# A decoder layer with routed experts on one core: rows of the modulation split between two engines, attention cut into pieces, half of one row moved into the routing, two output tiles lent to the weight stream

## The chip, the cores and the metric

The kernel runs on one core of a Trainium2 chip. The metric is the device time of one execution in microseconds (us); three runs gave 1640.99, 1641.44 and 1648.26 us, median 1641.44. What a run takes is decided by five engines with a queue each (TensorE, called PE in the profile; VectorE, DVE; ScalarE, ACT; GpSimd, POOL; SyncE, SP, which here only issues transfers) and by the 16 DMA engines that bring weights from memory.

## The reference, cut to what matters

One layer over 256 tokens of width 2048, all in float32:

```python
mod = (silu(c) @ ada_w + ada_b)                 # 6 rows of 2048
sh1, sc1, g1, sh2, sc2, g2 = split(mod, 6)
h = rmsnorm(x, norm1_g) * (1 + sc1) + sh1
x = x + g1 * hybrid_mixer(h)                    # h @ w_in -> heads -> @ w_out
h = rmsnorm(x, norm2_g) * (1 + sc2) + sh2
x = x + g2 * hierarchical_moe(h)                # 32 experts, 2 for each token
return rmsnorm(x, final_norm_g)
```

`hybrid_mixer` projects h to 5392 columns and feeds three groups of heads: a dilated-window attention (columns aq, ak, av), a gated delta rule with a short convolution (bq, bk, bv, a gate bz, and 16 gate columns bb, ba), and a grouped-query window attention (cq, ck, cv). Their outputs, side by side, go through `w_out`. Each expert is a gated MLP with two 2048x512 matrices in and one 512x2048 out, 12 MB of weights; all 32 experts are computed.

## The kernel before, in words

**Weights as a stream.** All big weights pass as tiles of 128 x 2048 float32 (1 MB) through rings of buffers. `Stream` (L114) keeps a queue of loads and a set of free slots: a load is issued on SP's queue when a slot is free (`pump`), the next tile is taken with `get`, and `done` frees its slot. `grow` adds slots, `retire` takes them out. There are two streams: `st` for nearly everything, and `st2`, with two slots, for the rows of the modulation that are needed later. The order of loads within a stream is the order of `add` (L472 to L484): the rest of the projection, the 16 tiles of `w_out`, then the 384 tiles of the experts. Each engine's instructions are put in order when the program is built, by a planner that follows the written order where nothing forces another; on the chip each queue runs strictly in order.

**First part.** The rows sh1 and sc1 and the columns bq, bk, bv are computed in six slices of the 2048 inputs (`SLICES`, L38): `ada_items` and `win_items` are merged, `win_tile` (L357) splits each float32 weight tile into a rounded half and a rest (`split`, L281: the rounding on ACT, the subtraction on DVE or POOL), multiplies in three products (`mm3`) and adds each slice's result to the sum in SBUF (`evac`, L267, on DVE). The 16 gate columns are multiplied there too (`gate_columns`, L370), tokens on the rows and 16 columns to stream.

**Second part.** All other columns, in pairs of 256 (`win_pair`, L391), use the finished h. In the written order come: `delta()` (L676), the long chain of the delta rule (conv, gates, a block inverse in six levels L812 to L842, states, outputs `ob`); then `use(merge(a_cols, rows_q[0:24]))`, `attention(0)`, the columns of c with 12 rows' tiles, `attention(1)`, and the columns bz with 20 (L937 to L941). `rows_q` are the 64 tiles of the rows g1, sh2, sc2 and g2, 16 each, multiplied on PE by `row_tile` (L425) in four groups of 32 output rows. Then `delta_out` (L885) and `wout_part` (L913), in two rounds of four.

**Routing and experts.** After `w_out`, x is normalised again, group and expert are chosen (L998 to L1055), and the chosen tokens are gathered by matrix products (`Slots`, L1083). The experts go in pairs: `hidden` (16 tiles a pair), `second` (8 tiles a pair), and `scatter` back into x. Slots of `st` in this stage: three of `ring1`, its two side slots (L951), four of `ring2` (L954), three of `ring3` (L1013) and the two buffers of `xa`, `h2` (L1061). `new_y` (L1211) takes four tiles of 128 x 1024 for the outputs of a pair.

What sets the room around the change:

```python
st.retire(*spare)            # L575
for s in side:
    st.retire(s, to=st2)
st.grow((wk, "rx"))          # one more slot until L947
...
st.grow(*slots(ring3, "rd", R4))                     # L1013
...
st.grow(*((cst, f"h2{b}") for b in range(NB)))       # L1061
```

Of the kernel before, what the change touches and what calls it, by code (L numbers as in the profile page):

```python
# [8 lines left out]
F32 = mybir.dt.float32  # L9
F32R = mybir.dt.float32r  # L10
# [6 lines left out]
P = 128  # L17
# [21 lines left out]

PAIRS = [c for a, e in ((O_AQ, O_BQ), (O_CQ, N_IN), (O_BZ, O_BB)) for c in range(a, e, 256)]  # L40

EARLY = ([("ada", s, k0, nk, q) for k0, nk in SLICES for s in range(2) for q in range(nk)]
         + [("b", k0, nk, c) for k0, nk in SLICES for c in range(O_BQ, O_BZ, 2048 // nk)]
         + [("pair", c, h) for c in PAIRS for h in range(2)]
# [4 lines left out]
def hybrid_moe(ctx: ExitStack, tc: tile.TileContext, x, c, norm1_g, norm2_g, early, ada_w, ada_b, w_bb,  # L49
# [154 lines left out]
    def win_items(j):  # L204
        k0, nk = SLICES[j]
        return [(early_load("b", k0, nk, c), lambda t, a=(k0, nk, c): win_tile(*a)(t)) for c in range(O_BQ, O_BZ, 2048 // nk)]

# [18 lines left out]
    for nk, r in ((4, 4), (2, 8)):  # L226
# [6 lines left out]
        for k0, n in SLICES:  # L233
            if n == nk:
# [10 lines left out]
    CH = [("aq0", 0, 2), ("aq1", 2, 2), ("ak0", 4, 2), ("ak1", 6, 2), ("bq", 8, 4), ("bk", 12, 4),  # L245
          ("bv0", 16, 4), ("bv1", 20, 4), ("cq0", 24, 2), ("cq1", 26, 2), ("ck", 28, 1)]
# [110 lines left out]
    def win_tile(k0, nk, c0):  # L357

        def chans(w, cc, m):

            h = hs[k0]
            p = bank("w")
            for u in range(2):
                for kt in range(nk):
                    mm3(p[:, 256 * u:256 * u + 256], [x[:, kt, cc + P * u:cc + P * (u + 1)] for x in w],
                        [x[:, kt] for x in h], kt == 0, kt == nk - 1)
            t, i = chan[m]
            evac(t[:, i:i + 2].rearrange("p m b t -> p (m b t)"), p, k0)

        def gate_columns():  # L370
            h = hs[k0]
            for b in range(NB):
                p = bank("w")
                for kt in range(nk):
                    mm3(p[:, 0:16], [x[:, kt, P * b:P * (b + 1)] for x in h], [x[:, k0 // P + kt] for x in wbb],
                        kt == 0, kt == nk - 1)
                evac(tok[:, b, K_BB:K_BB + 16], p[:, 0:16], k0)

        def f(t):
            t = t.rearrange("p (k n) -> p k n", k=nk)  # L380
            n = 1024 // nk
            for a in range(0, 2048 // nk, n):
                w = split(t[:, :, a:a + n], nk, 0)
                for z in range(0, n, 256):
                    chans(w, z, 8 + (c0 - O_BQ + a + z) // P)
            if c0 == O_BQ:
                gate_columns()
        return f
# [33 lines left out]

    rowp = {}

    def row_tile(i, kt):  # L425
        def f(t):
            if kt == 0:
                rowp[i] = bank("r", name="prow2")
            for g in range(4):
                mm(rowp[i][32 * g:32 * g + 32, :], csil[:, kt, 3 - i:35 - i], t[:, 512 * g:512 * (g + 1)],  # L430
                   start=(kt == 0), stop=(kt == 15))
# [18 lines left out]

    rows_q = [(ada_rows(i, kt), row_tile(i, kt)) for i in range(4) for kt in range(KT)]

# [16 lines left out]
    a_cols, c_cols, z_cols = ([x for c0 in range(a, e, 256) for x in on(st, win_pair(c0))]  # L469
                              for a, e in ((O_AQ, O_BQ), (O_CQ, N_IN), (O_BZ, O_BB)))  # L470
# [105 lines left out]
    for s in side:  # L576
        st.retire(s, to=st2)
    st.grow((wk, "rx"))
    use(first[-8:])
# [82 lines left out]
    def attention(grp):  # L662
        if grp:
            swap_keys()
            clo = ep_tile("av", 4, F32R)
        for j in range(2):
            ms = (2 * j, 2 * j + 1)
            sd = [attn_scores(grp, m) for m in ms]
            pair = (ep_tile(f"cq{j}", 2, F32R), clo[:, 2 * j:2 * j + 2]) if grp else \
                (ep_tile(f"aq{j}", 2, F32R), ep_tile(f"ak{j}", 2, F32R))  # L670
            for i, m in enumerate(ms):
                mix[m if grp == 0 else 12 + m] = tuple(t[:, i] for t in pair)
                attn_values(grp, m, *sd[i])


    def delta():  # L676
# [269 lines left out]
    g1hl = halves(scratch(dt=F32R), scratch(dt=F32R), mrow)  # L946
    st.retire((wk, "rx"))  # L947
# [341 lines left out]
    with tc.For_i(0, nov, 1):  # L1289
# [113 lines left out]
```

## Time and profile before

| | |
|---|---|
| median of three runs | 1641.44 us |
| profiled execution, whole | 1645.27 us |
| its span, first to last instruction | 1643.4 us |
| PE busy | 1545.9 us (94%) |
| DVE busy | 672.1 us (41%) |
| ACT busy | 398.6 us (24%) |
| POOL busy | 182.8 us (11%) |
| bytes moved | 573.76 MB, mean 349 GB/s |

An engine's busy time is the union of its instructions' times. A float32 product appears as two instructions, and products overlap in the array, so the mean duration of one is longer than the time between two: what a group costs is its busy time over its count. The line of a matrix product is always that of the helper `mm` (L65); what it belongs to is told by its output and input tiles.

### The profile page before, as it was taken

How to read it: one execution, taken by the hardware profiler on the slowest of the kernel's cores; microseconds unless marked ns; L12 is line 12 of the kernel's file. 1: busy time of each engine (PE TensorE's matmuls, PEld its weight loads, DVE VectorE, ACT ScalarE, POOL GpSimd, SP SyncE). 2: the span in 40 equal slices, each digit the busy share in tenths (PEclk: the TensorE clock that was granted, in tenths of full speed). 3: DMA queues.
4: the chain of work that ended last, by engine and by line, in shares of the span. 5: the costliest groups of instructions: out<-in, count | busy, mean ns of one | idle time of the engine just before them, and what ended most of it. 6: DMA issues, size and time to landing. Idle time of an engine off the chain costs nothing. (4 is left out here: it accounts for less than half of the span.)

```text
span 1643.4 us, 23829 instructions
## 1 busy us (share of the span) xinstructions
PE 1545.9 (94%) x10064; PEld 945.0 (58%) x10064; DVE 672.1 (41%) x1138; ACT 398.6 (24%) x683; POOL 182.8 (11%) x104
## 2 busy tenths in 40 slices
PE   5899899999999999799999999999999999999895
PEld 3678767898877667544544545445445445445433
DVE  3534854334433544423432533344244234235324
ACT  3323563344345334210110110111011101101102
POOL 1111222352222432000000000000000000000000
PEclk8999999999999999799999999999999999999998
DMA  9986457634589894699999999999999999999995
GB/s 392 408 329 237 162 206 293 246 155 161 225 309 315 308 369 178 232 397 421 420 419 421 421 420 421 421 420 420 421 420 421 420 421 421 421 421 421 420 420 218
DMA packets 82437, 573.76 MB, mean 349 GB/s; under 512 B 9740, under 2 KB 10100, under 8 KB 13336
## 3 DMA queue, kind: packets, MB, share of 16 engines
q1 hardware_dynamic: 82080, 572.02, 86.6%
q8 instruction: 81, 1.33, 0.3%
q10 hardware_dynamic: 248, 0.19, 0.0%
q14 instruction: 28, 0.23, 0.0%
HBM read 570.07 MB, written 2.10 MB: 348 GB/s over the span
## 5 line engine op out<-in xcount | busy, mean ns | idle before, releaser
L65 PE MATMUL u<-ring,xg 128*64 128x512 f32 x2048 | 485.9, 604 | 7.8 <-DMA ring<-in_expert_gu_dram 7.8
L65 PEld LDWEIGHTS u<-ring,xg 128*64 128x64 f32 x2048 | 134.3, 137 | 236.1 <-issue 190.5
L65 PE MATMUL d<-ring,hidT 128*64 128x256 f32 x2048 | 238.1, 382 | 10.5 <-DMA ring<-in_expert_dn_dram 8.9
L65 PE MATMUL w<-hx,stg 128*128 128x256 f32 x1392 | 197.1, 293 | 9.8 <-ACT stg L289 3.1
L65 PEld LDWEIGHTS w<-hx,stg 128*128 128x128 f32 x1392 | 176.6, 194 | 41.8 <-issue 24.3
L65 PEld LDWEIGHTS d<-ring,hidT 128*64 128x64 f32 x2048 | 144.0, 137 | 90.9 <-issue 10.3
L290 POOL TENSOR_TENSOR stg<-ring,stg 128x1024 fp32r<-128x1024 f32 x53 | 128.3, 2421 | 410.5 <-ACT stg L289 367.3
L289 ACT CAST stg<-ring 128x1024 fp32r<-128x1024 f32 x116 | 121.2, 1047 | 187.7 <-PE w L65 152.4
L1190 DVE TENSOR_TENSOR xt<-xt,s 128x512 f32<-128x512 f32 x120 | 82.6, 688 | 165.2 <-PE s L65 164.4
L290 DVE TENSOR_TENSOR stg<-ring,stg 128x1024 fp32r<-128x1024 f32 x63 | 82.2, 1306 | 104.5 <-ACT stg L289 103.7
L1174 DVE SCALAR_TENSOR_TENSOR z<-d,gs,g2b 64x512 f32<-64x512 f32 x120 | 90.0, 750 | 76.1 <-PE d L65 74.2
L65 PE MATMUL prow<-ring,csil 128*32 128x512 f32 (+1 forms) x896 | 113.3, 566 | 0.3 <-DVE csil L180 0.3
L1272 POOL TENSOR_TENSOR xf<-xt,fgb 128x1024 f32<-128x1024 f32 x1 | 2.4, 2377 | 954.9 <-SPq L1289 954.9
L1107 DVE TENSOR_TENSOR xg<-g,sh2c 128x512 f32<-128x512 f32 x64 | 43.6, 691 | 136.8 <-PE u L65 75.7
L65 PEld LDWEIGHTS w<-stg,hx 128*128 128x128 f32 x672 | 83.6, 189 | 22.3 <-issue 18.0
L65 PE MATMUL w<-stg,hx 128*128 128x256 f32 (+1 forms) x672 | 96.1, 288 | 0.0
L1146 ACT ACTIVATE hid<-u 64x512 f32<-64x512 f32 x32 | 18.9, 590 | 286.7 <-PE u L65 276.5
L65 PEld LDWEIGHTS s<-yah,wt 128*128 128x128 f32 x120 | 22.6, 188 | 97.6 <-issue 58.8
L1177 ACT CAST yah<-z 64x512 fp32r<-64x512 f32 x60 | 37.0, 617 | 166.8 <-DVE z L1174 166.8
L1147 DVE TENSOR_TENSOR hid<-hid,u 64x512 f32<-64x512 f32 x32 | 22.1, 690 | 134.0 <-ACT hid L1146 133.8
L65 PE MATMUL g<-oh,h2hi 128*128 128x256 f32 x256 | 70.2, 307 | 5.5 <-DVE xg L1107 4.8
L1121 ACT CAST wt<-t 128x512 fp32r<-128x512 f32 x16 | 9.4, 587 | 233.7 <-PE s L65 222.6
(387 smaller groups left out, 1704.6 us busy)
## 6 DMA issues: line engine op xcount, KB each, us to landing
ring<-in_expert_gu_dram SPq DMA_DIRECT2D x256, 1024.0 KB, 19.8
ring<-in_expert_dn_dram SPq DMA_DIRECT2D x128, 1024.0 KB, 19.8
ring<-in_early_dram SPq DMA_DIRECT2D x90, 1024.0 KB, 8.2
ring<-in_ada_w_dram SPq DMA_DIRECT2D x64, 1024.0 KB, 5.7
xt<-in_x_dram SPq DMA_DIRECT2D x8, 512.0 KB, 6.3
out_dram<-xt SPq DMA_DIRECT2D x8, 256.0 KB, 4.4
fgb<-in_final_norm_g_dram SPq DMA_DIRECT2D x1, 1024.0 KB, 19.8
rw<-in_router_w_dram SPq DMA_DIRECT2D x1, 320.0 KB, 5.2
```

Source lines behind the costliest of these rows:

```text
L65: return T.matmul(o, lhsT, rhs, start=start, stop=stop, skip_group_check=True)
L289: S.copy(hi, src)
L290: (G if nsplit[0] % GS[part] == GS[part] - 1 else V).tensor_tensor(lo, src, hi, op=ALU.subtract)
L1107: V.tensor_tensor(self.xg[:, 2 * q:2 * q + 2, 0:w], p[:, 0:2 * w].rearrange("p (k s) -> p k s", k=2), sh2c.rearrange("p n k -> p (n k)")[: ...
L1121: S.copy(self.wt.rearrange("p h b t -> p (h b t)"), p)
L1146: S.activation(hid[64:128], p[0:64], AF.Silu)
L1147: V.tensor_tensor(hid[0:64], hid[64:128], p[64:128], op=ALU.mult)
L1174: V.scalar_tensor_tensor(o.rearrange("p (n j) -> p n j", n=m), pd[q, 0:256 * m].rearrange("p (n j) -> p n j", n=m), gs[q, h, u:u + 1], g2h ...
L1177: S.copy(ys[h][q, c], o)
L1190: V.tensor_tensor(x1[n][:, b], x1[n][:, b], p, op=ALU.add)
L1272: G.tensor_tensor(xf, x1[0], fgb[:, None, 0:512].to_broadcast([P, NB, 512]), op=ALU.mult)
```

## The change

Four things.

1. The columns aq and ak join bq, bk and bv in the six slices; of `win_pair`'s columns av, cq, ck, cv and bz stay. The gate columns are multiplied the other way round (16 output rows, 256 tokens to stream) and turned back at the start of `delta`; cv is computed like ck and turned in `swap_keys`.
2. The rows g1 and sc2 (i = 0 and 2) are accumulated on DVE, tile by tile, into a buffer `racc`, and summed over the 128 rows by one set of four products at the end. The rows sh2 and g2 stay on PE. They alternate in the queue, and are spread evenly over the steps of the second part, among which `attention` now yields piece by piece. `racc` takes the room of the slot `rx`.
3. Of g2's 16 tiles the last 8 leave `st2`, and stand in `st` between `w_out` and the experts. They are multiplied after the routing is written, and g2 is spread over the tokens' rows behind the first expert's products instead of in `w_out`'s second round.
4. The expert outputs become two tiles of 8 KB a row in a pool of their own. Each serves `st` as a slot once, before it holds outputs.

```diff
-PAIRS = [c for a, e in ((O_AQ, O_BQ), (O_CQ, N_IN), (O_BZ, O_BB)) for c in range(a, e, 256)]
+PAIRS = [c for a, e in ((O_AV, O_BQ), (O_CQ, N_IN), (O_BZ, O_BB)) for c in range(a, e, 256)]
+SLICED = [(O_BQ, O_BZ), (O_AQ, O_AV)]
...
         def gate_columns():
             h = hs[k0]
-            for b in range(NB):
-                p = bank("w")
-                for kt in range(nk):
-                    mm3(p[:, 0:16], [x[:, kt, P * b:P * (b + 1)] for x in h], [x[:, k0 // P + kt] for x in wbb],
-                        kt == 0, kt == nk - 1)
-                evac(tok[:, b, K_BB:K_BB + 16], p[:, 0:16], k0)
+            p = bank("w")
+            for kt in range(nk):
+                mm3(p[0:16, 0:256], [x[:, k0 // P + kt] for x in wbb], [x[:, kt] for x in h], kt == 0, kt == nk - 1)
+            evac(bbT, p[0:16, 0:256], k0)
...
-    KINDS = [(O_AQ, O_AV, "chan", 0), (O_AV, O_BQ, "av", 0), (O_BQ, O_BZ, "chan", 8), (O_BZ, O_BB, "tok", K_BZ),
-             (O_CQ, O_CV, "chan", 24), (O_CV, N_IN, "tok", K_CV)]
+    KINDS = [(O_AV, O_BQ, "av", 0), (O_BZ, O_BB, "tok", K_BZ), (O_CQ, N_IN, "chan", 24)]
...
+        def on_dve(t):
+            if kt == 0:
+                rowp[i] = wk.tile([P, D], F32, name="racc", tag="racc")
+            acc = rowp[i]
+            for h in range(2):
+                c = slice(1024 * h, 1024 * (h + 1))
+                if kt == 0:
+                    V.tensor_scalar(acc[:, c], t[:, c], csil[:, kt, 3:4], None, op0=ALU.mult)
+                else:
+                    V.scalar_tensor_tensor(acc[:, c], t[:, c], csil[:, kt, 3:4], acc[:, c], op0=ALU.mult, op1=ALU.add)
             if kt == 15:
+                rowp[i] = bank("d", name="prow2")
+                for g in range(4):
+                    mm(rowp[i][32 * g:32 * g + 32, :], onec[:, 3 - i:35 - i], acc[:, 512 * g:512 * (g + 1)])
+        def f(t):
+            (on_pe if i % 2 else on_dve)(t)
+            if kt == (7 if i == 3 else 15):
                 V.tensor_tensor(mrow, mrow, rowp.pop(i), op=ALU.add)
...
-    rows_q = [(ada_rows(i, kt), row_tile(i, kt)) for i in range(4) for kt in range(KT)]
+    rows_q = [(ada_rows(i, kt), row_tile(i, kt)) for i0 in (0, 2) for kt in range(KT) for i in (i0, i0 + 1)
+              if i < 3 or kt < 8]
...
+    for kt in range(8, KT):
+        st.add(ada_rows(3, kt))
     for e in range(0, NE, 2):
...
-    st.grow((wk, "rx"))
     use(first[-8:])
...
-    use(merge(a_cols, rows_q[0:24]))
-    attention(0)
-    use(merge(c_cols, rows_q[24:36]))
-    attention(1)
-    use(merge(z_cols, rows_q[36:56]))
+    parts = [attention(grp) for grp in range(2)]
+    steps = a_cols + merge(c_cols, parts[:1] * 8) + merge(z_cols, parts[1:] * 8)
+    for step in merge(steps, rows_q[0:48]):
+        if isinstance(step, tuple):
+            use([step])
+        else:
+            next(step)
...
-        use(rows_q[56 + 2 * n:56 + 2 * n + 2])
+        use(rows_q[48 + 2 * n:48 + 2 * n + 2])
...
-        pg = bank("w")
-        spread2(pg, g1hl, 3, n)
-        S.copy(g2b[:, ns], pg)
...
+    for t in ("yh", "yl"):
+        st.grow((yp, t))
+        st.retire((yp, t))
...
+    p = bank("s", 1)
+    for kt in range(8):
+        t = st.get()
+        for g in range(4):
+            mm(p[32 * g:32 * g + 32, :], csil2[:, kt, 0:32], t[:, 512 * g:512 * (g + 1)], start=(kt == 0), stop=(kt == 7))
+        st.done()
+    g2r = mp.tile([P, 512], F32, name="g2r", tag="hid", bufs=1)
+    V.tensor_tensor(g2r, mrow, p, op=ALU.add)
+    g2hl = halves(*(mp.tile([P, 512], F32R, name="g2hl", tag="z") for _ in range(2)), g2r)
+
+    def spread_g2(n):
+        p = bank("s", 1)
+        spread2(p, g2hl, 3, n)
+        S.copy(g2b[:, 512 * n:512 * (n + 1)], p)
...
-    behind = []
+    behind = [lambda n=n: spread_g2(n) for n in range(4)]
...
-        yh, yl = new_y(F32R, "h"), new_y(F32R, "l")
+        yh, yl = new_y(F32R, "yh"), new_y(F32R, "yl")
```

## Rows read from the trace of the kernel before

**Rows 1.** The page: the span in 40 equal slices of 41 us; TensorE's granted clock and the share of the DMA engines in tenths, then GB/s.

```profile
PE   5899899999999999799999999999999999999895
PEclk8999999999999999799999999999999999999998
DMA  9986457634589894699999999999999999999995
GB/s 392 408 329 237 162 206 293 246 155 161 225 309 315 308 369 178 232 397 421 420 419 421 421 420 421 421 420 420 421 420 421 420 421 421 421 421 421 420 420 218
```

**Rows 2.** Busy time of each engine by stage (slices, second part, `w_out`, routing and first products, experts, end): length, busy us and instruction count of each engine, granted clock, DMA share, GB/s.

```profile
0.00:190.00 190.00, 163.05 (x1337) 130.66 (x1338) 88.06 (x168) 63.32 (x99) 29.43 (x25) 0.93 0.81 319
190.00:535.00 345.00, 339.31 (x2643) 272.87 (x2643) 149.16 (x273) 162.38 (x312) 107.83 (x60) 0.99 0.64 234
535.00:662.00 127.00, 125.81 (x614) 86.23 (x612) 58.16 (x70) 48.59 (x65) 42.88 (x18) 1.00 0.73 276
662.00:706.00 44.00, 34.44 (x166) 20.92 (x168) 18.10 (x51) 9.01 (x16) 0.24 (x1) 0.81 0.70 261
706.00:1618.00 912.00, 873.60 (x5246) 428.17 (x5242) 346.80 (x558) 108.90 (x178) 0.00 (x0) 0.99 1.01 420
1618.00:1644.00 26.00, 9.70 (x66) 6.14 (x64) 11.79 (x23) 6.43 (x14) 2.38 (x1) 0.77 0.36 113
```

**Rows 3.** TensorE's groups in the first 700 us, shapes kept apart: operation, out<-in, contraction rows * output rows, in partitions x elements, count, busy us, mean ns of one, idle before.

```profile
L65 PE MATMUL w<-hx,stg 128*128 128x256 f32 x1392 | 197.1, 293 | 9.8 <-ACT stg L289 3.1 <-DVE hx L352 2.8 <-DVE stg L290 1.5
L65 PE MATMUL prow<-ring,csil 128*32 128x512 f32 x640 | 90.8, 605 | 0.0
L65 PE MATMUL w<-wbb,hx 128*128 128x16 f32 x96 | 12.9, 259 | 0.0
L65 PE MATMUL w<-stg,hx 128*128 128x128 f32 x96 | 12.3, 276 | 0.0
L65 PE MATMUL w<-g1hl,identr 32*128 32x512 f32 x16 | 5.8, 441 | 0.0
```

**Rows 4.** DVE's and POOL's lines: durations of one in ns (least, median, most), first and last start, shape.

```profile
L1060 DVE SCALAR_TENSOR_TENSOR h2lo<-xa,r,h2hi x8: 735/748/752, 666.1 to 671.8; 128x512 fp32r<-128x512 f32 x8
L290 DVE TENSOR_TENSOR stg<-ring,stg x63: 1209/1225/3124, 26.7 to 652.7; 128x1024 fp32r<-128x1024 f32 x63
L931 DVE TENSOR_TENSOR xt<-xt,w 128x512 f32<-128x512 f32 x16 | 10.4, 679 | 0.0
L271 DVE TENSOR_TENSOR bq<-bq,w x10: 680/688/689, 56.8 to 182.2; 128x512 f32<-128x512 f32 x10
```

**Rows 5.** The chain of the delta rule and what ends beside it: lines with their durations, first and last start.

```profile
L691 ACT ACTIVATE ct<-bq,cw x4: 493/496/504, 183.0 to 184.2; 128x256 f32<-128x256 f32 x4
L803 DVE SCALAR_TENSOR_TENSOR R<-d,beta,qk x16: 336/341/351, 263.5 to 290.4; 128x128 f32<-128x128 f32 x16
L834 DVE TENSOR_TENSOR Tm<-Tm,d x20: 391/422/424, 305.6 to 379.2; 128x256 f32<-128x256 f32 x20
L880 DVE TENSOR_TENSOR ob<-ob,d x2: 671/680/689, 431.2 to 444.0; 128x512 f32<-128x512 f32 x2
L417 ACT COPY tok<-w x10: 257/367/378, 451.3 to 533.9; 128x256 f32<-128x256 f32 x8, 128x128 f32<-128x128 f32 x2
```

**Rows 6.** Busy time of three stretches, columns as in rows 2.

```profile
175.00:225.00 50.00, 44.19 (x321) 36.69 (x321) 39.62 (x73) 34.22 (x51) 12.12 (x7) 0.93 0.54 183
225.00:662.00 437.00, 433.61 (x3028) 332.77 (x3026) 180.18 (x290) 183.60 (x336) 141.73 (x73) 1.00 0.68 252
...
670.00:675.00 5.00, 0.00 (x0) 0.00 (x0) 4.73 (x23) 0.83 (x2) 0.00 (x0) 0.50 0.45 152
```

**Rows 7.** DVE operations of the chain and of the attention with two inputs in SBUF: durations as in rows 4.

```profile
L696 DVE SCALAR_TENSOR_TENSOR ct<-bv,cw,ct x24: 470/475/2597, 212.6 to 233.0; 128x255 f32<-128x255 f32 x8, 128x254 f32<-128x254 f32 x8, 128x253 f32<-128x253 f32 x8
L635 DVE SCALAR_TENSOR_TENSOR sc<-sc,cntA x16: 276/415/2274, 286.5 to 409.1; 128x128 f32<-128x128 f32 x8, 128x256 f32<-128x256 f32 x8
```

**Rows 8.** SP's queue: issues of expert loads around the routing (start, length of the merged piece, count).

```profile
600.25 0.43 SPq L191 DMA_DIRECT2D ring<-in_expert_gu_dram  x1
601.28 84.39 SPq L191 DMA_DIRECT2D ring<-in_expert_gu_dram  x14
653.99 0.33 SPq L191 DMA_DIRECT2D ring<-in_expert_gu_dram  x1
661.39 0.81 SPq L191 DMA_DIRECT2D ring<-in_expert_gu_dram  x2
671.91 0.99 SPq L191 DMA_DIRECT2D ring<-in_expert_gu_dram  x2
685.34 0.33 SPq L191 DMA_DIRECT2D ring<-in_expert_gu_dram  x1
```

**Rows 9.** The instructions in order of time in the routing: start, length, engine, line, out<-in, count, idle time before and what ended it.

```profile
666.58 1.93 PE L65 MATMUL d<-rw,xT 128*128 128x40 f32 x8 [0.75 <-ACT xT L993]
675.06 1.06 PE L65 MATMUL t<-Ae,before 128*128 128x32 f32 x4 [6.55 <-DVE Ae L1049]
677.33 0.58 PE L65 MATMUL g<-oh,h2hi 128*128 128x256 f32 x1 [0.78 <-DVE oh L1093]
683.37 3.65 PE L65 MATMUL u<-ring,xg 128*64 128x512 f32 x16
```

**Rows 10.** The tiles of the rows: TensorE's products on them between 450 and 535 us, and what SP's queue waited for before it could load them (us in total, times, longest).

```profile
L65 PE MATMUL prow<-ring,csil 128*32 128x512 f32 x136 | 18.1, 605 | 0.0
SPq L188 <- PE prow L65: 235.9, 56, 17.2
```

More of the change, by code (lines that the diff above doesn't have):

```diff
@@ L38 @@
 SLICES = [(0, 2), (256, 2), (512, 4), (1024, 4), (1536, 2), (1792, 2)]
-PAIRS = [c for a, e in ((O_AQ, O_BQ), (O_CQ, N_IN), (O_BZ, O_BB)) for c in range(a, e, 256)]
+PAIRS = [c for a, e in ((O_AV, O_BQ), (O_CQ, N_IN), (O_BZ, O_BB)) for c in range(a, e, 256)]
+SLICED = [(O_BQ, O_BZ), (O_AQ, O_AV)]
 EARLY = ([("ada", s, k0, nk, q) for k0, nk in SLICES for s in range(2) for q in range(nk)]
-         + [("b", k0, nk, c) for k0, nk in SLICES for c in range(O_BQ, O_BZ, 2048 // nk)]
+         + [("b", k0, nk, c) for k0, nk in SLICES for a, e in SLICED for c in range(a, e, 2048 // nk)]
          + [("pair", c, h) for c in PAIRS for h in range(2)]
@@ L180, in hybrid_moe @@
     V.tensor_copy(csil[:, :, 3], pt[:, 0:KT])
+    csil2 = cst.tile([P, 8, 36], F32, name="csil2")
+    V.tensor_copy(csil2, csil[:, 8:16])
     def early_load(*key):
@@ L205, in win_items @@
         k0, nk = SLICES[j]
-        return [(early_load("b", k0, nk, c), lambda t, a=(k0, nk, c): win_tile(*a)(t)) for c in range(O_BQ, O_BZ, 2048 // nk)]
+        return [(early_load("b", k0, nk, c), lambda t, a=(k0, nk, c): win_tile(*a)(t)) for s, e in SLICED for c in range(s, e, 2048 // nk)]
     def on(s, items):
@@ L245, in hybrid_moe @@
     CH = [("aq0", 0, 2), ("aq1", 2, 2), ("ak0", 4, 2), ("ak1", 6, 2), ("bq", 8, 4), ("bk", 12, 4),
-          ("bv0", 16, 4), ("bv1", 20, 4), ("cq0", 24, 2), ("cq1", 26, 2), ("ck", 28, 1)]
+          ("bv0", 16, 4), ("bv1", 20, 4), ("cq0", 24, 2), ("cq1", 26, 2), ("ck", 28, 1), ("cv", 29, 1)]
     chan = {}
     K_BZ, K_BB, K_CV = 0, 1024, 1040
-    KINDS = [(O_AQ, O_AV, "chan", 0), (O_AV, O_BQ, "av", 0), (O_BQ, O_BZ, "chan", 8), (O_BZ, O_BB, "tok", K_BZ),
-             (O_CQ, O_CV, "chan", 24), (O_CV, N_IN, "tok", K_CV)]
+    KINDS = [(O_AV, O_BQ, "av", 0), (O_BZ, O_BB, "tok", K_BZ), (O_CQ, N_IN, "chan", 24)]
     def ep_tile(tag, n, dt=F32):
@@ L259, in hybrid_moe @@
             chan[m0 + i] = (t, i)
+    bbT = ep.tile([P, 256], F32, name="bbT")[0:16]
     av = ep.tile([P, NB, 512], F32, name="av", tag="av")
@@ L384, in f @@
                 for z in range(0, n, 256):
-                    chans(w, z, 8 + (c0 - O_BQ + a + z) // P)
+                    chans(w, z, (c0 + a + z) // P - (O_BQ // P - 8 if c0 >= O_BQ else 0))
             if c0 == O_BQ:
@@ L423, in hybrid_moe, with on_pe @@
     rowp = {}
+    onec = ep.tile([P, 36], F32, name="onec")
+    V.memset(onec, 0.0)
+    V.memset(onec[:, 3:4], 1.0)
     def row_tile(i, kt):
-        def f(t):
+        def on_pe(t):
             if kt == 0:
@@ L430, in f @@
                 mm(rowp[i][32 * g:32 * g + 32, :], csil[:, kt, 3 - i:35 - i], t[:, 512 * g:512 * (g + 1)],
-                   start=(kt == 0), stop=(kt == 15))
-            if kt == 15:
+                   start=(kt == 0), stop=(kt == (7 if i == 3 else 15)))
+        def on_dve(t):
[8 more added lines that the diff above has]
+                    V.scalar_tensor_tensor(acc[:, c], t[:, c], csil[:, kt, 3:4], acc[:, c], op0=ALU.mult, op1=ALU.add)
+            if kt == 15:
+                rowp[i] = bank("d", name="prow2")
[4 more added lines that the diff above has]
+            if kt == (7 if i == 3 else 15):
                 V.tensor_tensor(mrow, mrow, rowp.pop(i), op=ALU.add)
@@ L469, in hybrid_moe @@
     a_cols, c_cols, z_cols = ([x for c0 in range(a, e, 256) for x in on(st, win_pair(c0))]
-                              for a, e in ((O_AQ, O_BQ), (O_CQ, N_IN), (O_BZ, O_BB)))
+                              for a, e in ((O_AV, O_BQ), (O_CQ, N_IN), (O_BZ, O_BB)))
     w_items = [(early_load("out", n, q), None) for qs in ((0, 3), (1, 2)) for n in range(4) for q in qs]
@@ L593, in swap_keys @@
     def swap_keys():
+        p = bank("a")
+        for b in range(NB):
+            T.transpose(p[:, P * b:P * (b + 1)], head(29)[:, b], ident)
+        S.copy(tok[:, :, K_CV:K_CV + 128], p[:, 0:256].rearrange("p (b n) -> p b n", b=NB))
         kd = wk.tile([P, NB, P], F32, name="kswap")
@@ L667, in attention @@
             ms = (2 * j, 2 * j + 1)
-            sd = [attn_scores(grp, m) for m in ms]
+            sd = []
+            for m in ms:
+                sd.append(attn_scores(grp, m))
+                yield
             pair = (ep_tile(f"cq{j}", 2, F32R), clo[:, 2 * j:2 * j + 2]) if grp else \
@@ L673, in attention @@
                 attn_values(grp, m, *sd[i])
+                yield
     def delta():
@@ L701, in delta @@
         conv(1)
+        pt = bank("d")
+        for b in range(NB):
+            T.transpose(pt[:, 16 * b:16 * (b + 1)], bbT[:, P * b:P * (b + 1)], ident[0:16, 0:16])
+        V.tensor_copy(tok[:, :, K_BB:K_BB + 16], pt[:, 0:32].rearrange("p (b n) -> p b n", b=NB))
         bb = tok[:, :, K_BB:K_BB + 8]
@@ L946, in hybrid_moe @@
     g1hl = halves(scratch(dt=F32R), scratch(dt=F32R), mrow)
-    st.retire((wk, "rx"))
     for n in range(4):
         wout_part(n, (0, 3), g1hl, tmp.tile([P, 2, 384], F32, name="g1s", tag="pT").rearrange("p u s -> p (u s)")[:, 0:512])
-        use(rows_q[56 + 2 * n:56 + 2 * n + 2])
+        use(rows_q[48 + 2 * n:48 + 2 * n + 2])
     st.grow(*side)
@@ L1014, in hybrid_moe @@
     mp = ctx.enter_context(tc.tile_pool(name="moe", bufs=2, side="right", reuse_waits="tile"))
+    yp = ctx.enter_context(tc.tile_pool(name="yp", bufs=1, side="right", reuse_waits="tile"))
+    for t in ("yh", "yl"):
+        st.grow((yp, t))
+        st.retire((yp, t))
     psum = ctx.enter_context(tc.tile_pool(name="mps", bufs=1, space=bass.MemoryType.PSUM, reuse_waits="tile"))
@@ L1204, in squares @@
             if n == 3 and b:
-                y = mp.tile([P, 1024], F32, name="sqv", tag="yal", bufs=1)[:, 0:512]
+                y = new_y(F32, "yl")[0][:, 0:512]
                 V.scalar_tensor_tensor(y, x1[n][:, b], 0.0, x1[n][:, b], op0=ALU.add, op1=ALU.mult, accum_out=ss3[:, b, n:n + 1])
@@ L1211, in new_y @@
     def new_y(dt, s):
-        return tuple(mp.tile([P, 1024], dt, name=f"y{h}{s}", tag=f"y{h}{s}", bufs=1) for h in "ab")
+        t = yp.tile([P, 2, 1024], dt, name=s, tag=s)
+        return t[:, 0], t[:, 1]
     ovn, ovs, ove = small("ovn", [P, NE]), small("ovs", [P, NE]), small("ove", [P, NE])
@@ L1272, in scaled @@
         G.tensor_tensor(xf, x1[0], fgb[:, None, 0:512].to_broadcast([P, NB, 512]), op=ALU.mult)
-    ys = new_y(F32, "h")
+    ys = new_y(F32, "yh")
     for n in range(4):
@@ L1314, in hybrid_moe @@
         sl.back(0)
-        ys = new_y(F32, "h")
+        ys = new_y(F32, "yh")
         G.memset(ys[0][64:128], 0.0)
```

## Prediction

> **What bounds the kernel now.** I read the page's 40 slices first, then the busy time by stage, then TensorE's groups, and last SP's issues around the routing. The reader is to see two kernels in one. From about 706 us to 1618 us the DMA engines run at 420 GB/s without a gap [rows 1, 2]: a tile of 1.049 MB every 2.495 us, and no engine's work there can move the end unless it stops the stream. Before 662 us it is TensorE: from 190 to 662 us it is busy 465.1 of 472 us while DMA has a share of 0.64 and 0.73 [rows 2]. Between the two, from 662 to 706 us, neither is full: DMA has 0.70 [rows 2], because 14 slots are filled by 672.9 us and the next load is issued only at 685.34 us, when the first expert tile has been used [rows 8]. So the end is the moment at which `w_out` is done (R, 662 us), plus the loads still to come, plus the gaps in them. The change works on all three.
>
> **The sum, on TensorE before R.** Costs per instruction are busy time over count [rows 3].
>
> Rows g1 and sc2 leave TensorE: 32 tiles of 8 instructions at 90.8/640 = 0.142 us, 36.3 us. The two final sums bring back 2 x 8 x 0.142 = 2.3 us. Net -34.0.
>
> Half of g2's row leaves: 8 tiles of 8 instructions, -9.1.
>
> The gate columns: 96 products of 16 columns cost 12.9 us, 48 of 256 columns take their place. No row shows 16 output rows; the nearest, 128 output rows and 256 columns, is 197.1/1392 = 0.142 us, so 6.8 us. With 0.3 us of transposes, -5.8. Bounds: the 96 old ones halved (6.5) and twice the price (13.6), -6 to +1.
>
> cv: 96 products of 128 columns, 12.3 us, become 48 of 256, 6.8 us, and 0.3 us of transposes, -5.2.
>
> g2's spread: half of a group of 16, 5.8/2, -2.9; it goes behind the first expert's products, in the DMA-bound stage.
>
> The columns aq and ak move and don't shrink: 4 pairs x 96 products x 0.142 = 54.4 us go from the second part into the slices. There 8 more tiles are loaded, 20 us of DMA in a stage of 190 us with a share of 0.81 [rows 2], and DVE adds 20 sums of 0.69 us [rows 4], 14 us where it is busy 88 of 190. I cost both at nothing; without that cover they would be 20 us.
>
> Sum: -34.0 - 9.1 - 5.8 - 5.2 - 2.9 = -57.0 us.
>
> **What it costs on DVE.** 64 operations over 1024 columns with two inputs in SBUF. No row shows this one. The subtraction of the same shape takes 1.225 us, and an operation with a column of factors 0.748 against 0.679 us at 512 columns [rows 4], so 1.225 + 0.07 = 1.29 us, 83 us in all. DVE's load between the slices and R was 207 us of 472 [rows 2]; it becomes about 280 of 366. That alone still fits. What counts is who stands behind them in DVE's queue. The chain of the delta rule begins with the first convolution at 183.0 and ends with the last `ob` at 444.7, 261.7 us, while the gate's last columns came at 533.9 [rows 5]: 89 us of cover. Afterwards the chain starts at 183.0 + 54.4 - 5.8 = 231.6 and would end at 493; the columns end at 533.9 - 5.8 - 5.2 - 36.3 + 1.1 (32 of 56 rows' tiles fewer on TensorE in this stretch, one final sum) = 488. The cover is gone, and what lengthens the chain is late in `delta_out` and after it. By the code 118 of its steps are DVE's (48 convolution taps, 28 where the blocks are set up, 24 in the levels, 4 of scaling, 14 in the last loop). 48 of the 64 row operations are spread over this stretch, 48 x 1.29 / 257 = 24% of the time; a step finds one in its way that often and waits half of it, 0.155 us, 118 times: 18 us. Bounds: nothing, or a gain of a few us, if the chain is shorter with less other work on TensorE, which was 100% busy beside it; and 12% of 366 us, 43 us, from the stretch in which DVE was busy 39.6 of 50 us and TensorE lost 5.8 [rows 6]. I take 18, near the middle: in the rest of the stage, with DVE at 41%, TensorE lost only 3.4 of 437 us [rows 6].
>
> In this case's rows an operation of DVE with two SBUF inputs, 0.475 or 0.415 us as a rule, took up to 2.597 and 2.274 us [rows 7], which is about a POOL subtraction longer. The Trainium skill (SBUF — State Buffer, Who interferes with whom) says that such an operation and a GpSimd one that reads SBUF exclude each other, and the second blocks fully. The trace agrees for single ones. All 64 row operations have two SBUF inputs but the first of each row, and POOL is busy 151 of 472 us [rows 2], so by the rule a third of them would wait some 1.2 us, 25 us more on DVE, and the 18 us would be 24; but the subtraction on DVE, with the same two inputs, shows a median of 1.225 us against a least of 1.209 [rows 4], so I leave the sum at 18.
>
> **What the loads cost.** Before, nine expert tiles were issued by 654 us, three at 661 to 662, two at 672 [rows 8]. Now eight of the first nine slots hold g2's tiles: 8 more expert tiles are to come after R, +19.9 us. Against it the gap closes: at R there are five slots (three of `ring3`, two of the outputs), at R + 10 two more, and the eight of g2 as TensorE takes them in its idle 6.55 us before the ranks and 0.78 us before the gather [rows 9]. Five and two tiles keep DMA busy for 17.5 us, the eight for 20 more. So the 44 us at 0.70 become full: -44 x (1 - 0.70/1.01) = -13.5 us. The two lent slots are what bridges R + 12.5 to R + 17.5; their worth, 5 us, is inside this. Net +6.4. Bounds: +19.9 if the gap stays, -13.5 if g2's tiles are used before R and their slots are free for experts. g2's products need 9.1 us in 7.3 us of idle time, twice that at the granted clock of 0.50 (1.2 GHz) that the idle TensorE has at 670 us [rows 6]; the first expert would start 2 to 11 us later after R, behind which the loads wait for nothing, since 16 slots are there. I cost that at nothing.
>
> Total: -57.0 + 18 + 6.4 = -32.6 us. The profiled execution took 1645.3 us, of which 1643.4 are span, and would take 1612.7; the median is 3.8 us lower, so 1609 us.
>
> **Rivals.** (a) DVE's queue costs nothing: -57.0 + 6.4, 1591 us. For it speaks that DVE has 86 us to spare and TensorE's other work can fill the waits; against it the lost cover. (b) The two slots of `st2` pace the rows. Before, 136 products are 17 tiles in 85 us, 5.0 us each, and SP waited 4.2 us for the slot, 56 times [rows 10]; 48 tiles at 5.0 us are 240 us in a stretch of 257, but a tile that DVE uses is held 2.6 us and not 1.1, and if it waits behind other work, 6 us each make 288 us: 31 over, and SP's queue holds the other loads behind. With TensorE's own small loss, -57 + 6.4 + 34, 1625 us; with the 18 as well, 1640. (c) The end on the other side: DVE's strict order makes the chain the bound. If the row operations stand ahead of every DVE step, half a one each time, 118 x 0.645 = 76 us: -57 + 6.4 + 76, 1667 us. It decides from 0.43 us a step, 51 us in all; for it speaks that a row operation takes three times a level's step of 0.42 us [rows 5], against it that they cover a quarter of the stretch. (d) Part three doesn't do what it says: g2's tiles are used late, their slots come late and the gap stays at 13.5 us: 1622 us; that lies within the forecast's own range.
>
> **How the numbers follow.** The forecast with (d) gets 0.57 (1594 to 1624), (a) 0.20, (b) 0.13, (c) 0.10. About 0.5% is what a measurement of this kernel can tell from no change, so faster is below 1633.2 and slower above 1649.6. Faster: 0.57 + 0.20 + half of (b), 0.83. Within: the other half of (b) and the low end of (c), 0.08. Slower: 0.09. The range reaches from 1582, a little below (a) where the chain shortens, to 1637, which leaves out the upper end of (b) and (c).
>
> **What would show it.** Right: the first convolution near 232 us, `ob` complete near 511, `w_out` done near 624, and from there DMA at 1.0 without the gap at the first expert; no products of `prow` for g1 and sc2. The DVE part is wrong if TensorE's idle time in the second part is under 5 us (then (a)) or the chain takes over 300 us (then (c)); SP waiting over 6 us for each row's tile would show (b). The load part is wrong if DMA still falls under 0.9 between R and the first expert. The prediction fails as a whole if TensorE's busy time before R is not some 57 us shorter, or if the expert stage no longer runs at 420 GB/s.

## The result, and the profile after

The changed kernel took 1657.7 us (median of five, 1655.96 to 1659.2) against 1641.44 us: the ratio is 1.0086, with a 95% interval of 1.0062 to 1.0110. The prediction was 1609 us, faster, with a range of 1582 to 1637. It was wrong in sign.

The page of the changed kernel, the same lines as [rows 1], with DVE's; a slice is 41.4 us:

```profile
PE   5999989999993599999999999999999999999995
...
DVE  3455689853255654423532443344244234235324
...
PEclk8999999999995699999999999999999999999998
DMA  9997686762147884999999999999999999999995
GB/s 394 374 356 257 238 304 242 294 223 104 61 151 281 291 319 151 376 420 420 420 420 421 420 420 420 420 420 420 420 420 420 420 420 420 420 420 420 421 420 213
```

The reader is to see a hole that the kernel before did not have: TensorE at 3 and 5 tenths in the 13th and 14th slice, and, ahead of it, DMA at 2, 1 and 4 tenths in the 10th to 12th slice. The stages, columns as in [rows 2] (slices; the delta rule; from its end to the first use of g1; `w_out`; routing and first products):

```profile
0.00:211.00 211.00, 189.10 (x1578) 152.33 (x1582) 108.10 (x186) 76.33 (x110) 39.72 (x29) 0.97 0.83 323
211.00:495.00 284.00, 273.80 (x2082) 235.19 (x2080) 179.54 (x297) 153.38 (x300) 103.64 (x56) 0.98 0.54 196
495.00:554.00 59.00, 19.32 (x80) 4.74 (x80) 29.90 (x36) 2.76 (x6) 1.04 (x1) 0.53 0.77 278
554.00:669.00 115.00, 106.66 (x450) 77.67 (x450) 67.99 (x78) 39.40 (x52) 34.74 (x14) 0.95 0.68 250
669.00:706.00 37.00, 33.98 (x198) 17.97 (x200) 18.83 (x52) 10.01 (x19) 0.24 (x1) 0.91 1.00 401
```

In the 59 us from 495 to 554 us TensorE is busy 19 us, at a granted clock of 0.53, near the lower of its two levels (0.50, 1.2 GHz); DVE is busy 30 us and no other engine more than 3. The last row is the routing, and there DMA has 1.00, against 0.70 before [rows 2]: that part came as forecast. The instructions in order of time around the hole say what happens:

```profile
342.33 1.27 DVE L447 SCALAR_TENSOR_TENSOR racc<-ring,csil,racc 128x1024 f32<-128x1024 f32 x1
...
492.43 1.05 PE L67 MATMUL d<-t,qk 128*128 128x128 f32 x8
493.41 1.06 PE L67 MATMUL prow<-racc,onec 128*32 128x512 f32 x8
496.22 0.67 DVE L456 TENSOR_TENSOR mrow<-mrow,prow 128x512 f32<-128x512 f32 x1
496.82 1.40 DVE L445 TENSOR_SCALAR racc<-ring,csil 128x1024 f32<-128x1024 f32 x2
499.54 1.94 PE L67 MATMUL prow<-ring,csil 128*32 128x512 f32 x8 [5.06 <-DVE mrow L456]
...
553.84 0.69 DVE L456 TENSOR_TENSOR mrow<-mrow,prow 128x512 f32<-128x512 f32 x1 [2.93 <-PE prow L67]
554.62 0.62 ACT L463 CAST t<-mrow 128x512 fp32r<-128x512 f32 x1 [43.65 <-DVE mrow L456]
```

DVE has finished row 0 in `racc` at 343.6 us. Its sum over the 128 rows (`prow<-racc,onec`) comes 150 us later, at 493.41, right behind the last product of the delta rule (`d<-t,qk`). Until then `racc` is taken, so row 2 can't begin, and row 1's bank `r` is taken as well, since row 1 is added to `mrow` after row 0 (498.8 us); so row 3 can't begin either. The first tiles of rows 2 and 3 are used at 496.82 and 499.54 us. By then all other work of the second part is done, and `w_out`'s first round needs g1 out of `mrow`, which is read only after row 3's sum: ACT waits 43.65 us for it.

### The profile page after: what moved, and what is told of

It is laid out like the page before. It is cut to its first block, busy times and chain, and to the rows that moved or that the text cites. A ratio compares the mean times of both kernels' runs of the same rounds, so it can differ in the third digit from the quotient of the medians.

```text
span 1654.1 us, 23250 instructions
## 1 busy us (share of the span) xinstructions
PE 1511.8 (91%) x9732; PEld 922.3 (56%) x9732; DVE 763.3 (46%) x1226; ACT 397.7 (24%) x679; POOL 181.8 (11%) x101
## 5 line engine op out<-in xcount | busy, mean ns | idle before, releaser
L67 PE MATMUL w<-hx,stg 128*128 128x256 f32 x1440 | 189.9, 286 | 8.6 <-DVE aq L275 4.2
L1235 ACT CAST yh<-z 64x512 fp32r<-64x512 f32 x120 | 74.0, 616 | 269.2 <-DVE z L1232 269.2
L67 PE MATMUL prow<-ring,csil 128*32 128x512 f32 (+1 forms) x576 | 81.7, 598 | 40.0 <-DMA ring<-in_ada_w_dram 34.6
L447 DVE SCALAR_TENSOR_TENSOR racc<-ring,csil,racc 128x1024 f32<-128x1024 f32 x60 | 84.4, 1446 | 34.0 <-DMA ring<-in_ada_w_dram 33.9
L67 PEld LDWEIGHTS s<-yh,wt 128*128 128x128 f32 x240 | 45.0, 187 | 94.7 <-issue 59.5
L67 PE MATMUL w<-stg,hx 128*128 128x256 f32 x576 | 89.9, 300 | 0.2 <-DVE stg L294 0.2
L1236 DVE TENSOR_TENSOR yl<-z,yh 64x512 fp32r<-64x512 f32 x120 | 82.2, 685 | 3.1
L67 PEld LDWEIGHTS w<-stg,hx 128*128 128x128 f32 x576 | 76.1, 197 | 11.2 <-issue 8.7
```

The source lines that it names most:

```text
L67: return T.matmul(o, lhsT, rhs, start=start, stop=stop, skip_group_check=True)
L447: V.scalar_tensor_tensor(acc[:, c], t[:, c], csil[:, kt, 3:4], acc[:, c], op0=ALU.mult, op1=ALU.add)
L1235: S.copy(ys[h][q, c], o)
L1236: V.tensor_tensor(yl[h][q, c], o, ys[h][q, c], op=ALU.subtract)
```

## The experiments

The table gives, for each kernel, the median, the time of the one execution that was profiled, and from its profile the first convolution and the last `ob` of the delta rule, R (the start of the last addition after `w_out`), and what follows R. The profiled execution lies up to 7.4 us from its kernel's median (e8), while what follows R differs by some 4 us between all of them; so a difference of R of less than some 8 us is read together with the medians. Ratios are to the kernel before measured beside each kernel, with medians of 1641.44 to 1645.41 us.

| kernel | median us | profiled us | delta rule | R | end - R |
|---|---|---|---|---|---|
| before | 1641.44 | 1645.27 | 183.0 to 444.0 | 661.9 | 981.5 |
| changed | 1657.7 | 1655.96 | 211.3 to 495.0 | 669.4 | 984.7 |
| e1, bank a | 1611.69 | 1611.9 | 210.0 to 501.4 | 625.3 | 984.7 |
| e2, row 3 late | 1654.36 | 1655.6 | 212.2 to 501.0 | 668.7 | 985.2 |
| e3, rows on TensorE | 1625.71 | 1631.18 | 211.6 to 487.8 | 645.3 | 984.2 |
| e4, gap alone | 1642.82 | 1642.38 | 182.1 to 443.4 | 654.8 | 985.6 |
| e6, bank w | 1615.71 | 1615.75 | 211.8 to 503.0 | 629.8 | 984.2 |
| e7, row order | 1615.09 | 1614.14 | 209.1 to 497.8 | 627.7 | 984.6 |
| e8, short DVE work | 1590.4 | 1597.8 | 207.7 to 491.5 | 611.1 | 984.9 |
| e9, g2 not moved | 1613.74 | 1610.75 | 211.5 to 507.1 | 627.3 | 981.6 |
| e10, third slot | 1653.0 | 1655.14 | 212.5 to 499.2 | 670.0 | 983.4 |

**e1: the sum in another bank.** A bank of tag d is one of three that the delta rule uses throughout, and the tiles of a tag are handed out in written order; `delta()` is written ahead of all rows.

```diff
-                rowp[i] = bank("d", name="prow2")
+                rowp[i] = bank("a", name="prow2")
```

> The changed kernel with one word changed: the bank that takes the final sum of a row accumulated on DVE is tag a (the attention's) instead of tag d (the delta rule's). Theory A (the sum of row 0 waits for a bank of d until the delta rule is over at 493 us, racc stays taken, 24 tiles of rows 2 and 3 then come alone through two slots, and w_out's first round waits for mrow until 554 us): the sum comes before 420 us, no stretch of 25 us before w_out has TensorE under 20 us busy except at the start, and the time falls by 40 to 60 us, to 1600 to 1618. Rival B (two slots of the rows' stream and DVE's load pace the rows whatever the bank): the rows' tiles still end after 560 us and the time stays at 1645 to 1665. Rival C (DVE's queue lengthens the delta chain as rows now meet its levels): the chain ends after 515 us and the time is 1625 to 1645.

Measured: 1611.69 us, ratio to before 0.9797 (0.9768 to 0.9827). The lines of the sum in the changed kernel, then in e1 (durations, first and last start), and the stretch that was the hole, both with the stretch ahead of it:

```profile
L67 PE MATMUL prow<-racc,onec x16: 592/604/617, 493.4 to 594.2; 128*32 128x512 f32 x16
400.00:495.00 95.00, 94.47 (x735) 85.88 (x733) 41.53 (x67) 52.53 (x115) 40.92 (x23) 1.00 0.30 105
495.00:554.00 59.00, 19.32 (x80) 4.74 (x80) 29.90 (x36) 2.76 (x6) 1.04 (x1) 0.53 0.77 278
```

```profile
L67 PE MATMUL prow<-racc,onec x16: 592/604/617, 409.3 to 548.0; 128*32 128x512 f32 x16
400.00:495.00 95.00, 95.00 (x744) 79.75 (x743) 58.56 (x82) 49.62 (x116) 36.12 (x19) 1.00 0.68 255
495.00:554.00 59.00, 48.91 (x215) 34.77 (x214) 52.42 (x56) 18.58 (x25) 20.71 (x11) 0.91 0.73 267
```

The sum comes at 409 us, the rows flow again between 400 and 495 us (DMA 0.68 instead of 0.30), and TensorE has 30 us more work in the 59 us that were the hole. R falls by 44.1 us; what follows R does not change. Theory A holds; one figure was too strict, the 25 us from 500 with 19.5 us of TensorE instead of 20. Rivals B and C fail: the last row is added at 548.7 us with the same two slots, and the chain ends at 501.4. e1 is also faster than both kernels.

**e6: a third bank, as a control.**

```diff
-                rowp[i] = bank("d", name="prow2")
+                rowp[i] = bank("w", name="prow2")
```

> The changed kernel with the final sum in a bank of tag w (the projection's) instead of d. Theory A (what costs is that a bank of d comes free only when the delta rule ends): like bank a, 1605 to 1618. Rival (it is the attention's bank, or another order of the attention that bank a brings, which helped): 1640 to 1660.

Measured: 1615.71 us, 0.9836 (0.9810 to 0.9863). The line of the sum:

```profile
L67 PE MATMUL prow<-racc,onec x16: 592/592/617, 386.7 to 562.7; 128*32 128x512 f32 x16
```

The sum comes at 386.7 us. So it is leaving d that counts, and not the attention's bank. Even so the sum does not come at once in either bank: DVE has finished row 0 at 345.7 us in e1 and at 345.9 in e6, so it still waits 64 and 41 us, and in e1 the DMA share is 0.34 from 350 to 410 us. Whether a bank of its own would bring more was not run.

**e2: the wait of g1 taken away, the bank left.**

```diff
-                V.tensor_tensor(mrow, mrow, rowp.pop(i), op=ALU.add)
+                if i < 3:
+                    V.tensor_tensor(mrow, mrow, rowp.pop(i), op=ALU.add)
...
     g1hl = halves(scratch(dt=F32R), scratch(dt=F32R), mrow)
+    V.tensor_tensor(mrow, mrow, rowp.pop(3), op=ALU.add)
```

> The changed kernel with bank d as it is; only row 3's sum is added to mrow after g1 has been read from it, so that w_out's first round no longer waits for row 3's last tile. Theory A: row 0's sum stays at about 493 us and the rows' last tile near 590, but w_out's first round starts near 500 instead of 556; TensorE is filled, and the time falls by 20 to 40 us, to 1615 to 1638. If the wait of g1 for mrow were not what keeps TensorE idle (rival: the rows alone pace it), the time stays above 1650.

Measured: 1654.36 us, 1.0069 (1.0046 to 1.0092). A miss in the time: it falls where the rival, that the rows alone pace it, had put it. The stretches from 500 us:

```profile
500.00:575.00 75.00, 62.95 (x272) 41.21 (x265) 58.13 (x61) 21.68 (x27) 19.87 (x10) 0.89 0.84 304
575.00:618.00 43.00, 7.73 (x36) 3.24 (x34) 24.59 (x22) 2.28 (x3) 2.34 (x1) 0.60 0.74 276
618.00:669.00 51.00, 49.25 (x234) 37.72 (x233) 24.07 (x34) 18.90 (x30) 13.34 (x6) 0.97 0.55 207
```

`w_out`'s first round does start at 508.7 us, as expected. The hole moves: from 575 to 618 us TensorE waits for row 2, whose sum is added at 615.8 us and which the second round's g1 and n2 are read after. The wait of g1 in the changed kernel was where the lateness showed, not its cause. The cause lies ahead of it, in the 24 tiles of rows 2 and 3 that can only start when the delta rule is over; from there on, as the rival says, they pace the end.

**e10: a third slot for the late rows.**

```diff
     for step in merge(steps, rows_q[0:48]):
+        if step is rows_q[34]:
+            st2.grow((wk, "qk"))
```

> The changed kernel with bank d as it is, and a third slot for the rows' stream from the 35th row tile on (the buffer qk of the delta rule, which is over by then). If the 16 tiles of rows 2 and 3 that come after the delta rule, 57 us at 3.6 us a tile, are paced by two slots, three bring them to the DMA's 2.5 us a tile, 40 us, and the time falls by 8 to 20 us, to 1638 to 1650, while row 0's sum stays at about 493 us. If DVE, or the strict order of the queues, paces them: 1653 to 1661.

Measured: 1653.0 us, 1.0048 (1.0030 to 1.0065). That is the low end of the second expectation; but the kernel before, measured beside it, took 1645.41 us, and 1.0048 times 1641.44 is 1649.3, in the first. So it is inconclusive as a test in time. The trace shows the stretch of the 16 tiles, from row 2's first to row 3's last, shorter by 7 us (45.5 instead of 52.3 us between the first and the eighth of row 3's tiles), and the reason why it isn't shorter still:

```profile
525.00:550.00 25.00, 6.52 (x28) 0.80 (x32) 9.92 (x8) 0.00 (x0) 0.00 (x0) 0.50 0.95 331
```

With three slots the DMA engines are full, 0.95, but move 331 GB/s: a tile in 3.2 us, not in 2.5. Of these 7 us, 4.2 were lost at the start, since the delta rule ended later (499.2 instead of 495.0 us; the sum came at 497.6): g1 is read from `mrow` at 552.1 instead of 554.6 us. R is 670.0 us, so the rest went in `w_out`; why is open.

**e3: the DVE part undone.**

```diff
-            (on_pe if i % 2 else on_dve)(t)
+            on_pe(t)
...
-    rows_q = [... for i0 in (0, 2) for kt in range(KT) for i in (i0, i0 + 1)
+    rows_q = [... for i in range(4) for kt in range(KT)
               if i < 3 or kt < 8]
```

> The changed kernel with the DVE part undone: all four rows on TensorE, one after the other (row 0, 1, 2, half of 3), everything else as changed. Theory A: no racc, no sum, no hole; TensorE has 34 us more work than in a changed kernel without a hole: 1615 to 1632. Rival B (the two slots pace the rows): like the changed kernel, 1645 to 1665. If the slices with aq and ak or the attention in pieces were what costs time: above 1641.

Measured: 1625.71 us, 0.9890 (0.9864 to 0.9915), in the middle of theory A's range. The stretch that was the hole:

```profile
495.00:554.00 59.00, 53.98 (x306) 35.73 (x302) 25.84 (x31) 26.69 (x46) 20.17 (x8) 0.91 0.81 301
```

The slices with aq and ak, the attention in pieces and the moves into the routing are together a gain by themselves; with the sum in bank d the DVE part turns it into a loss, and in bank a it adds 14 us of gain (1625.71 - 1611.69).

**e4: parts three and four alone.** The kernel before with the last eight tiles of g2's row in `st`, `spread_g2` behind the first expert, and `yh`, `yl` lent.

> The kernel before with parts 3 and 4 alone: half of g2's row in st before the experts, g2 spread behind the first expert, the output tiles lent as slots. By the sum: -9.1 - 2.9 us of TensorE before w_out ends and +6.4 us of loads, so -5.6: 1636, 1630 to 1642. If the gap at the routing stays open: 1641 to 1650. If the lent slots or g2's late half cost time by themselves: above 1650.

Measured: 1642.82 us, 0.9995 (0.9978 to 1.0011): no difference, just past the end of what the sum expected and within the rival's 1641 to 1650, an open gap. In the profiled executions R came 7.1 us earlier, not 12.0, and what follows R 4.1 us longer; that of the kernel before lay 3.8 us above its median, so the gain in R is nearer 3 us. The routing in e4:

```profile
655.00:706.00 51.00, 47.69 (x252) 22.41 (x254) 19.15 (x52) 13.12 (x22) 0.24 (x1) 0.93 0.99 404
```

DMA at 0.99 there: the gap of [rows 2] is closed, so the rival's reason is not the one, and the eight tiles that came into it use it up.

**e9: g2's half put back, the rest as e1.** In `rows_q` all 16 tiles of row 3, none in `st`; g2's halves are taken from `mrow`.

```diff
-              if i < 3 or kt < 8]
+              ]
...
-    for kt in range(8, KT):
-        st.add(ada_rows(3, kt))
```

> Bank a, and part 3 undone but for the place of g2's spread: all 16 tiles of g2's row with the other rows; the output tiles are still lent. By the sum: 9 us more of TensorE before w_out ends; from there to the end 8 tiles fewer (-19.9 us) and a gap of about 13.5 us less the 5 us of the lent slots: 976 to 978 us instead of 984.7. Together 1611 to 1615, no difference. If the half in the routing is worth its 9 us without a price: 1618 to 1622.

Measured: 1613.74 us, 0.9828 (0.9801 to 0.9856); beside e1 no difference, as expected, but by another sum: R is 2.0 us later in the profiled executions, some 5 by the medians, and not 9, and what follows R is 981.6 us, as in the kernel before, and not 976 to 978. The routing in e9:

```profile
627.00:671.00 44.00, 37.34 (x164) 22.85 (x166) 18.92 (x52) 11.87 (x21) 0.24 (x1) 0.77 0.70 268
```

The gap is as open as before, at 0.70. So the 5 us that I had given to the two lent slots are not seen where g2's tiles don't pass through.

**e8: what DVE's work costs.**

```diff
-                c = slice(1024 * h, 1024 * (h + 1))
+                c = slice(1024 * h, 1024 * (h + 1) if kt == 0 else 1024 * h + 16)
...
-                rowp[i] = bank("d", name="prow2")
+                rowp[i] = bank("a", name="prow2")
```

> Bank a, and each row operation on DVE after the first of its row reads 16 columns instead of 1024 (rows 0 and 2 are left out but for a part); all loads, waits and TensorE's work as they were. It measures what the 83 us of DVE work cost. Theory A (18 us by waits in DVE's queue): 15 to 20 us less than with bank a alone, 1590 to 1597. Rival (DVE's load is hidden, the loss is elsewhere): 1607 to 1614.

Measured: 1590.4 us, 0.9681 (0.9654 to 0.9707): 21.3 us less than e1, at the edge of theory A's range in time and 1.3 us past its 15 to 20. The row operation in e8 and two stretches, then the same stretches in e1:

```profile
L447 DVE SCALAR_TENSOR_TENSOR racc<-ring,csil,racc x60: 219/229/2469, 194.4 to 530.2; 128x16 f32<-128x16 f32 x60
200.00:350.00 150.00, 144.10 (x1082) 121.36 (x1081) 103.03 (x222) 88.04 (x154) 44.37 (x23) 0.97 0.74 275
500.00:550.00 50.00, 47.86 (x200) 34.88 (x199) 32.13 (x45) 17.82 (x22) 17.62 (x8) 0.96 0.76 291
```

```profile
200.00:350.00 150.00, 141.27 (x1008) 117.80 (x1008) 130.21 (x208) 82.92 (x141) 48.15 (x21) 0.93 0.73 270
500.00:550.00 50.00, 39.91 (x164) 27.18 (x163) 46.46 (x48) 15.66 (x21) 14.21 (x7) 0.90 0.72 254
```

In e1 DVE is busy 130 of these 150 us, and again 46 of 50 from 500 us, and in both TensorE falls behind: by 2.8 us in the first and by 8.0 in the second, where `w_out`'s first round stands among the row operations.

**e7: the same work in another order.**

```diff
-    ... for i0 in (0, 2) for kt in range(KT) for i in (i0, i0 + 1)
+    ... for row in ((1,), (0, 3), (2,)) for kt in range(KT) for i in row
               if i < 3 or kt < 8]
...
-                rowp[i] = bank("d", name="prow2")
+                rowp[i] = bank("a", name="prow2")
```

> Bank a, and the rows in another order: row 1 alone on TensorE first, then row 0 (DVE) beside the half of row 3, then row 2 (DVE). No tile and no operation is added or left out. If DVE's full load between 200 and 350 us (20 to 25 of 25 us) costs TensorE its idle time there, moving the row operations behind it gives back 5 to 12 us: 1598 to 1607. If it is the number of row operations, not their place: 1608 to 1616. If 24 tiles on DVE in a row are paced by two slots: over 1620.

Measured: 1615.09 us, 0.9826 (0.9784 to 0.9868). It falls into the second case. The stretches of e7:

```profile
200.00:350.00 150.00, 146.30 (x1128) 119.86 (x1126) 108.36 (x198) 84.31 (x149) 46.18 (x25) 1.00 0.67 245
350.00:500.00 150.00, 141.20 (x1084) 122.46 (x1084) 116.64 (x133) 72.55 (x156) 64.66 (x33) 0.99 0.69 252
500.00:550.00 50.00, 33.41 (x116) 22.94 (x116) 43.53 (x42) 12.25 (x16) 12.31 (x4) 0.84 0.68 248
```

From 200 to 350 us TensorE gains 5.0 us beside e1 (146.30 busy instead of 141.27), from 350 to 500 us it loses 8.8 (e1 is busy all 150), and from 500 to 550 us 6.5 (33.41 instead of 39.91): in this order the loss moves to a later place and does not get smaller.

## Why the prediction was wrong

**The step that failed** is "The two final sums bring back 2 x 8 x 0.142 = 2.3 us." I priced the sum as work, did not ask where it writes, and so put the wait for that place at nothing. It takes a bank of tag d behind all banks of the delta rule, so that row 0, finished at 343.6 us, keeps `racc` until the sum at 493.4 us: a wait of 150 us. After that 16 of the 24 tiles of rows 2 and 3 come with nothing beside them. R came out at 669.4 us; with the sum elsewhere it is 625.3, and the sum of the prediction (662 - 57 + 18) is 623. e1 is thus near what I forecast for the changed kernel: 1612 us against 1609. That the two lie so close is in part luck, since the three terms were each off by some us and the errors partly cancel. The code to see the wait stood in the diff.

**The TensorE sum of 57.0 us.** R in e8, where DVE's work is all but gone, is 50.8 us earlier than before in the profiled executions; with each R moved by what its execution differs from the median, some 54. By parts, with the figure so moved in brackets: the rows' 34.0 was 34.2 (36), e3 to e8; the gate columns and cv, 11.0, with the slices and the attention in pieces, 9.5 (15), e4 to e3; g2's half and spread, 12.0, 7.1 (3), before to e4. The parts are thus known to some 5 us, the sum better; g2's half gave less than its 9.1 in e9 too, and why is open. The moved columns, costed at nothing, show no cost in e4 to e3. But the first convolution came at 211.3, not 231.6 us, for a reason that I had not seen: the last sums of aq and ak stand behind it, at 235.0 and 237.6 us, with 120 of the 1152 products of the slices, 16.3 us.

**The 18 us on DVE.** By medians it is 21.3 us (e1 to e8), by R of the profiled executions 14.2. The number came near, the path only in part. I had it as a delay of the chain's steps; but the chain is only 7.6 us longer in e1 than in e8 (291.4 and 283.8 us), and TensorE's larger loss lies in the stretch behind it, 8.0 us from 500 to 550. In all kernels with rows on DVE the chain took 284 to 296 us instead of 261. With DVE's row work all but gone it still took 283.8, and with the rows on TensorE 276.2 (e3): most of its lengthening has another cause, which no run isolates. A row operation took 1.276 us where I had 1.29:

```profile
L447 DVE SCALAR_TENSOR_TENSOR racc<-ring,csil,racc x60: 1254/1276/3447, 196.1 to 589.2; 128x1024 f32<-128x1024 f32 x60
L447 DVE SCALAR_TENSOR_TENSOR racc<-ring,csil,racc 128x1024 f32<-128x1024 f32 x60 | 84.4, 1446 | 34.0 <-DMA ring<-in_ada_w_dram 33.9
328.87 4.65 DVE L447 SCALAR_TENSOR_TENSOR racc<-ring,csil,racc 128x1024 f32<-128x1024 f32 x2
329.78 2.66 POOL L294 TENSOR_TENSOR stg<-ring,stg 128x1024 fp32r<-128x1024 f32 x1 [8.83 <-ACT stg L293]
```

The longest, 3.447 us, is 2.17 us over the median, as the longest of [rows 7] were some 2.1 and 1.9 over theirs. In the changed kernel's trace 7 of the 60 took 1.42 us or more, and each of these 7 started while an operation of POOL with its inputs in SBUF was running; the other 53 took 1.285 us at most, also the 8 during which such an operation of POOL began. The last two lines show one such pair of row operations, 4.65 us instead of some 2.5, with POOL's subtraction in it. This fits the rule of the Trainium skill (SBUF — State Buffer, Who interferes with whom), that a DVE operation with two SBUF inputs and a GpSimd one that reads SBUF exclude each other; no run took POOL's work away to show it. The mean is 1.446 us, 0.17 over the median and not the 0.4 that a third of the operations waiting 1.2 us would give.

**The 6.4 us of loads.** What follows R was 3.2 us longer in the changed kernel, and 1.9 to 4.1 in all kernels with g2's half in the routing. The mechanism was right, eight more tiles and a closed gap, but the term was twice too large, and the share of the lent slots in it is not seen (e9).

**The rivals.** (b) came nearest: the rows are late, behind two slots. But I had it as a pace of the slots all through the second part, 31 us. e1 has the same two slots and not this hole, and SP's waits in the changed kernel are short of the 6 us a tile that I had named as (b)'s sign:

```profile
SPq L192 <- PE prow L67: 78.9, 23, 14.6
SPq L192 <- DVE racc L447: 72.6, 23, 6.6
```

That is 3.3 us a wait, less than the 4.2 of [rows 10]. (a) is refuted by e8, where DVE's work is worth 21 us, and (c) by the chain, 291 us in e1, with 7.6 of it from DVE's row work. (d) is refuted by DMA at 1.00 after R. The sign of failure that I had named, a TensorE that is not busy some 57 us less before R, did come: 588.9 us of busy time before R instead of 628.2, 39 less. It does not point at the hole, though: in e1, without it, TensorE is busy 583.3 us, 45 less.

## What to carry to other kernels

Work that is moved to another engine still ends in a shared room: for each new buffer ask which tag it is drawn from, who holds that tag in written order, and what stays taken until it is free. The late accumulator showed here as a transfer stream that ran dry (DMA at 1 tenth) some 40 to 80 us ahead of the idle engine, so look for the cause before the hole, not only in it. When one wait is taken away and the time stays, as in e2, see where the idle time went before giving up the theory.

## What the runs showed of the hardware

Rows of `ada_w`, 8 KB for each partition out of rows of 32 KB, kept the DMA engines 0.95 busy at 331 GB/s (e10), where the experts' tiles run at 420 GB/s and 1.01 [rows 2]. The same stretch with two slots (changed) and with three (e10):

```profile
520.00:545.00 25.00, 7.04 (x32) 0.80 (x32) 8.88 (x8) 0.00 (x0) 0.00 (x0) 0.50 0.74 268
520.00:545.00 25.00, 7.74 (x32) 0.80 (x32) 10.44 (x9) 0.00 (x0) 0.00 (x0) 0.50 0.96 343
```

By proportion either is an estimated 360 GB/s for fully busy engines (268/0.74 and 343/0.96), so the number of slots does not explain the difference to the experts' tiles; whether the distance of the pieces in memory does, no run shows. I had reckoned 2.5 us for every tile.

The first operation of a row on DVE, with one tensor input, took a median of 0.744 us for 1024 columns, against 1.276 with two; its longest was 2.900 us.

```profile
L445 DVE TENSOR_SCALAR racc<-ring,csil x4: 739/744/2900, 184.8 to 497.5; 128x1024 f32<-128x1024 f32 x4
```
